# A transformer layer with product-key experts: the selection of two token blocks placed beside the start of the dense expert stage

## The chip, the cores and the metric

The kernel runs on one core of a Trainium2 chip. The metric is the device time of one execution in microseconds (us). The profile is that of one execution; its times count from the start of its span. The engines are TensorE (PE; its weight loads PEld), VectorE (DVE), ScalarE (ACT), GpSimd (POOL) and SyncE (SP), which here only issues DMA transfers.

## The reference

One layer over 1024 tokens of width 1024: two attentions (differential and chunked) whose gated outputs are merged and added to `x`, giving `h`; then a retrieval of experts; then a final norm.

```python
h = h + merged @ w_out
# peer(), on rmsnorm(h), for each token and each of 8 heads
s1, s2 = q[:, :, 0] . keys[:, 0], q[:, :, 1] . keys[:, 1]     # 128 keys each
v1, i1 = top_k(s1, 16);  v2, i2 = top_k(s2, 16)
sc, ci = top_k(v1[..., :, None] + v2[..., None, :], 16)
e = i1[ci // 16] * 128 + i2[ci % 16]                           # one of 16384 experts
g = softmax(sc)
a = gelu(u[e] . xb) * g
out = rmsnorm(h + sum(a * v[e]))
```

So every token uses 8 x 16 of 16384 experts, each a row of `u` and a row of `v`.

## The kernel before, in words

The 1024 tokens are eight blocks of 128. The front (projections, attentions, merge, queries) ends in `merge`, which leaves for each block the 16 best keys of either half (`vv`, `iu`), and in `choose` (called through `sel`), the *selection*: it adds the values to candidates (`cand`), takes the best 16 with `top16` (L558, on VectorE), and looks up the indices with one-hot products (`ohib`: a ScalarE cast at L611, VectorE at L612 to L619). Its exponential (L623) and small casts (`pf` at L587, `pos` at L602) run on ScalarE. For the blocks of `SBLK` it ends in `ei` (L639), the list of expert numbers.

The experts are done in two ways. For blocks 2 to 5 (`DBLK`) `dense_experts` computes all experts. The 16384 experts are 128 chunks of 128. It first transposes the normed tokens `xd` (L697, into the PSUM tile `trd`) and splits them into a high and a low part `x2h`, `x2l` (helper `split`, L126 on ScalarE and L127 on VectorE). For each chunk it loads a tile of `u` (`wr` in `wtile`) and one of `v` (`vr`), splits both (`wh`, `wl`, `vh`, `vl`), forms `ph` with 24 matmuls (`mm3`, L134), applies Gelu (L756), multiplies by the gate (`gj`, L757), splits the product (`ah`, `al`) and adds 24 more matmuls to the sums (`second` L710, `fourth` L717). `ph` has one buffer, `wh` and `wl` have two each. The gates have been written to DRAM tile by tile (`gst` to `gdr`, L673) by `gates`, and come back as `gj`, 16 transfers for four chunks. The end adds the sums to `h` (`hx`, L778) and applies the final norm (`final`, with the weights `wfd`).

For blocks 0, 1, 6 and 7 (`SBLK`) `experts` gathers 128 rows of `u` and 128 of `v` for each block by indirect DMA on GpSimd (L804), with one VectorE instruction for each (L810, L816). The dense stage and the gathers stand beside each other.

A scheduler puts the instructions of each engine into one fixed order, by the order in which the program states them and by when their inputs and their memory are free in its model of time. Engines wait for each other through semaphores. Memory comes from pools: a tile of a pool that is opened later can use the room of closed pools only when the last user of the tiles there is done. The pools `yza` and `tkp` (tiles of the selection), `fc`, `sm` and `psp` are in `fstack`; the end of the program reads:

```python
        with pool("gk") as gk:
            weave(mop(2, mp, yzb), 26, (gates(gk, d1), 32 * len(d1)))
            weave(mop(3, mp, yza), 26, (chain(sel([4, 5], yzb), gates(gk, d2)), 18 + 32 * len(d2)))
    run(sel([6, 7], yza))
    fstack.close()
    dense_experts()
    for b in SBLK:
        experts(b)
```

Of the kernel before, what the change touches and what calls it, by code (L numbers as in the profile page):

```python
# [7 lines left out]
F32 = mybir.dt.float32  # L8
# [7 lines left out]
P = 128  # L16
D = 1024
S = 1024
NB = S // P
KC = D // P  # L20
# [5 lines left out]
NCH = 128  # L26
# [6 lines left out]
DBLK = [2, 3, 4, 5]  # L33
# [33 lines left out]
def chain(*gens):  # L67
    for g in gens:
        yield from g
# [3 lines left out]
def layer_kernel(ctx, tc, x, w1, w_in, b_gate, lq1, lk1, lq2, lk2, subln, rel,  # L73
                 w_bd, w_bc, w_out, w2, wq, keyst, u, v, ut, wf, identd, dmd, iotad, out):
    nc = tc.nc
# [2 lines left out]
    gp = ctx.enter_context(tc.tile_pool(name="gath", bufs=GBUFS))  # L78
    sms = ctx.enter_context(tc.tile_pool(name="sms", bufs=2))
    wp = ctx.enter_context(tc.tile_pool(name="wp", bufs=2))  # L80
    drp = ctx.enter_context(tc.tile_pool(name="dr", bufs=1, space=bass.MemoryType.DRAM))

    def load(pool, shape, src, name):
# [53 lines left out]
    dsel = {}  # L137

    fstack = ExitStack()
    yza = fstack.enter_context(tc.tile_pool(name="yza", bufs=1))  # L140
    tkp = fstack.enter_context(tc.tile_pool(name="tkp", bufs=1))
    fc = fstack.enter_context(tc.tile_pool(name="fcon", bufs=1))
    sm = fstack.enter_context(tc.tile_pool(name="sm", bufs=4))
    psp = fstack.enter_context(tc.tile_pool(name="ps", bufs=2, space=PSUM))
# [536 lines left out]
    def dense_experts():  # L681
# [3 lines left out]
        with ExitStack() as st:  # L685
# [41 lines left out]
                    fourth(1, chunks)  # L727
                    chunks.clear()

            wfb = dk.tile([P, D], F32, name="wfd", bufs=1)  # L730
            nc.sync.dma_start(wfb, wf.to_broadcast([P, D]))
            hxs = []
            chunks = []
            new = None
            for j in range(NCH):
                if j == NCH - 2:
                    for b in DBLK[:2]:
                        hx = dk.tile([P, D], F32, name="hx", tag="hx", bufs=2)
                        nc.sync.dma_start(hx, hd[b])
                        hxs.append(hx)  # L740
                uw = wtile(ut[j])
                vr = dk.tile([P, D], F32, name="vr", tag="vr", bufs=RBUFS)
                nc.sync.dma_start(vr, v[j * P:(j + 1) * P, :])
                vh = dk.tile([P, D], F32R, name="vh", tag="vh", bufs=VBUFS)
                vl = dk.tile([P, D], F32R, name="vl", tag="vl", bufs=VBUFS)
                for hf in range(2):
                    cs = slice(hf * 512, hf * 512 + 512)
                    split(vr[:, cs], vh[:, cs], vl[:, cs])
                if j % JG == 0:
                    gj = dk.tile([P, T // TB, JG, TB], F32, name="gj", tag="gj")  # L750
                    for i in range(T // TB):
                        nc.sync.dma_start(gj[:, i], gdr[i][:, j:j + JG, :])
                ph = pd.tile([P, 512], F32, name="ph", tag="ph")
                mm3(ph, uw, (xh, xl), KC)
                ge = dk.tile([P, T], F32, name="ge", tag="ge")
                nc.scalar.activation(ge, ph, AF.Gelu)  # L756
                nc.vector.tensor_mul(ge.rearrange("p (n t) -> p n t", t=TB), ge.rearrange("p (n t) -> p n t", t=TB),  # L757
                                     gj[:, :, j % JG, :])
                ah = dk.tile([P, T], F32R, name="ah", tag="ah", bufs=ABUFS)
                al = dk.tile([P, T], F32R, name="al", tag="al", bufs=ABUFS)  # L760
                split(ge, ah, al)
                if new:
                    chunks.append(new)
                    sums(chunks)
                new = (j, (ah, al), (vh, vl))
            chunks.append(new)
            sums(chunks)
            for i, b in enumerate(DBLK):
# [120 lines left out]
    with pool("yzb") as yzb, pool("mp") as mp:  # L889
# [4 lines left out]
        with pool("gk") as gk:  # L894
            weave(mop(2, mp, yzb), 26, (gates(gk, d1), 32 * len(d1)))
            weave(mop(3, mp, yza), 26, (chain(sel([4, 5], yzb), gates(gk, d2)), 18 + 32 * len(d2)))
    run(sel([6, 7], yza))
    fstack.close()
    dense_experts()
    for b in SBLK:  # L900
        experts(b)
# [51 lines left out]
```

## Time and profile before

| | |
|---|---|
| median of three runs | 3437.65 us (3435.08 to 3438.16) |
| profiled execution | 3433.26 us, span 3431.5 us |
| mean granted TensorE clock in it | 0.944 |
| TensorE busy | 3085.0 us (90%) |
| VectorE busy | 2700.0 us (79%) |
| ScalarE busy | 1446.3 us (42%) |
| GpSimd busy | 1249.1 us (36%) |
| DMA, mean over the span | 288 GB/s |

The busy times are sums over the whole span, and stages with different limits are mixed in them, so the stretches of time are looked at one by one. A row of a timeline gives the start, the duration, the engine, the line, the tiles written and read, the shapes and, in brackets, how long the engine was idle before and what released it. Consecutive instructions overlap by a little, so the distance between two starts can be shorter than a duration. On SP's queue the duration is that of a row of issues, not of the transfers.

### The profile page before, as it was taken

To read this page: it belongs to the slowest core of one execution; us is meant where nothing else is said; L and a number is where in the kernel's file an instruction comes from. 1 tells how busy PE (TensorE), PEld (TensorE's weight loads), DVE (VectorE), ACT (ScalarE), POOL (GpSimd) and SP (SyncE) were. 2 spreads that over 40 slices of the span, in tenths; PEclk is the share of its full clock that TensorE was granted. 3 is DMA by queue.
4 is the path that set the end of the run, shared out by engine and by line. 5 is a ranking of instruction groups with operands and counts; after the bars stand their busy time and mean duration, and the time that the engine had idled before them with its cause. 6 is when DMAs were issued, how large, how long until landed. Compare 5 with 4: busy or idle time off the path is not lost.

```text
span 3431.5 us, 48288 instructions
## 1 busy us (share of the span) xinstructions
PE 3085.0 (90%) x16032; PEld 2551.8 (74%) x16032; DVE 2700.0 (79%) x5848; ACT 1446.3 (42%) x3029; POOL 1249.1 (36%) x1028
## 2 busy tenths in 40 slices
PE   7987699999979886987798359999999999999998
PEld 7986578888857654676677348888888888888886
DVE  4436897777779899987976978889998888999543
ACT  5634433434423544567669523333233333333332
POOL 0000455555544522344000144555555555555000
PEclk9999899999989987998898669999999999999999
DMA  7675999999999975898544499999999999999531
GB/s 240 219 244 189 374 333 348 333 352 334 326 340 351 324 236 186 281 360 331 203 162 157 145 343 319 346 350 339 347 345 345 346 342 344 346 340 349 166 123 49
DMA packets 406122, 987.13 MB, mean 288 GB/s; under 512 B 43184, under 2 KB 188400, under 8 KB 403696
## 3 DMA queue, kind: packets, MB, share of 16 engines
q0 software_dynamic: 147456, 536.94, 44.1%
q1 hardware_dynamic: 258416, 447.11, 37.4%
q8 instruction: 126, 2.06, 0.2%
q14 instruction: 124, 1.02, 0.1%
HBM read 905.72 MB, written 78.15 MB: 287 GB/s over the span
## 4 chain that ended last, share of the span: by engine, by line
PE 71%; issue 12%; DVE 7%; DMA 7%; ACT 2%; POOL 1%; SPq 0%; DVEq 0%; POOLq 0%; ACTq 0%
PE ph L134 20%; PE mm L134 16%; PE acc L710 15%; PE acc L717 5%; PE mm L490 5%; PE sc L347 3%; PE pv L372 3%; PE tr L203 2%; DMA ge<-in_u_dram,ei 2%; DVE junk L810 1%; DVE p L353 1%; POOL ge L804 1%; DMA rb<-rst 1%; DMA ge<-in_v_dram,ei 1%; DVE acc L816 1%
## 5 line engine op out<-in xcount | busy, mean ns | idle before, releaser
L804 POOL DMA_INDIRECT ge<-in_u_dram,ei x512 | 619.1, 1209 | 1249.0 <-DVE junk L810 396.4
L804 POOL DMA_INDIRECT ge<-in_v_dram,ei x512 | 629.8, 1230 | 683.2 <-DVE acc L816 462.0
L816 DVE SCALAR_TENSOR_TENSOR acc<-ge,a,acc 128x1024 f32<-128x1024 f32 x512 | 655.1, 1280 | 26.2 <-DMA ge<-in_v_dram,ei 20.1
L810 DVE SCALAR_TENSOR_TENSOR junk<-ge,xs 128x1024 bf16<-128x1024 f32 x512 | 624.7, 1220 | 53.7 <-DMA ge<-in_u_dram,ei 45.7
L127 DVE TENSOR_TENSOR wl<-wr,wh 128x1024 fp32r<-128x1024 f32 x232 | 283.6, 1223 | 233.1 <-ACT wh L126 107.5
L126 ACT CAST wh<-wr 128x1024 fp32r<-128x1024 f32 x232 | 243.7, 1051 | 406.5 <-PE ph L134 267.1
L134 PE MATMUL ph<-x2h,wh 128*128 128x512 f32 x1024 | 400.3, 391 | 11.8 <-ACT wh L126 10.4
L134 PE MATMUL ph<-x2l,wh 128*128 128x512 f32 x1024 | 399.9, 390 | 0.0
L134 PE MATMUL mm<-xh,wh 128*128 128x256 f32 (+1 forms) x1248 | 372.0, 325 | 0.7 <-ACT st L286 0.5
L134 PE MATMUL mm<-xl,wh 128*128 128x256 f32 (+1 forms) x1248 | 366.8, 321 | 1.4 <-DVE xl L232 1.3
L134 PEld LDWEIGHTS mm<-xh,wh 128*128 128x128 f32 x1248 | 236.9, 190 | 24.8 <-ACT st L286 2.3
L134 PE MATMUL ph<-x2h,wl 128*128 128x512 f32 x1024 | 253.1, 389 | 0.0
L134 PEld LDWEIGHTS mm<-xl,wh 128*128 128x128 f32 x1248 | 236.4, 190 | 21.5 <-DVE xl L232 2.1
L126 ACT CAST vh<-vr 128x512 fp32r<-128x512 f32 x256 | 140.4, 619 | 264.8 <-PE acc L717 243.4
L134 PE MATMUL mm<-xh,wl 128*128 128x256 f32 (+1 forms) x1248 | 234.4, 323 | 0.0
L134 PEld LDWEIGHTS ph<-x2h,wh 128*128 128x128 f32 x1024 | 193.2, 189 | 52.9 <-ACT wh L126 10.8
L134 PEld LDWEIGHTS ph<-x2l,wh 128*128 128x128 f32 x1024 | 193.2, 189 | 40.2
L134 PEld LDWEIGHTS ph<-x2h,wl 128*128 128x128 f32 x1024 | 192.3, 188 | 40.0
L347 PE MATMUL sc<-kt,qt 64*128 64x256 f32 (+3 forms) x608 | 202.1, 533 | 17.8 <-DVE mn L353 10.2
L710 PE MATMUL acc<-vh,ah 128*128 128x512 f32 x768 | 198.3, 389 | 0.0
L126 ACT CAST ah<-ge 128x512 fp32r<-128x512 f32 x128 | 79.7, 622 | 281.4 <-DVE ge L757 266.3
L134 PEld LDWEIGHTS mm<-xh,wl 128*128 128x128 f32 x1248 | 184.7, 189 | 16.8
(199 smaller groups left out, 5741.6 us busy)
## 6 DMA issues: line engine op xcount, KB each, us to landing
vr<-in_v_dram SPq DMA_DIRECT2D x128, 512.0 KB
wr<-in_ut_dram SPq DMA_DIRECT2D x128, 512.0 KB
wr<-in_w_in_dram SPq DMA_DIRECT2D x104, 512.0 KB
gdr<-gst SPq DMA_DIRECT2D x16, 2048.0 KB
gj<-gdr SPq DMA_DIRECT2D x512, 64.0 KB
wr<-in_w_bd_dram SPq DMA_DIRECT2D x40, 512.0 KB
wr<-in_w_out_dram SPq DMA_DIRECT2D x40, 512.0 KB
wr<-in_wq_dram SPq DMA_DIRECT2D x40, 512.0 KB
```

The lines of the kernel that those rows point to most:

```text
L126: nc.scalar.copy(hi, raw)
L127: nc.vector.tensor_sub(lo, raw, hi.bitcast(F32))
L134: nc.tensor.matmul(o, w[a][:, k, :], xx[b][:, k, :], start=(i == 0), stop=(i == last))
L203: nc.tensor.transpose(o[:, i * P:(i + 1) * P], s, ident)
L347: nc.tensor.matmul(o[:, :k1 - k0], q, k[:, k0:k1], start=True, stop=True)
L372: nc.tensor.matmul(o[:, :P], aT[:, j - c, :], vt[:, v0 + j, :], start=(j == 0), stop=(j == n - 1))
L490: nc.tensor.matmul(o, w[:, k, :], xx[:, k, :], start=(k == 0), stop=(k == K - 1))
L710: nc.tensor.matmul(acc[i][hf], a[x][:, i * P:(i + 1) * P], b[y][:, hf * 512:hf * 512 + 512], **kw)
L717: nc.tensor.matmul(o, aa[:, 3 * P:4 * P], bb[:, cs], start=(n == 0), stop=(n == len(todo) - 1))
L804: nc.gpsimd.indirect_dma_start(out=t, out_offset=None, in_=src, in_offset=bass.IndirectOffsetOnAxis(ap=ei[:, k:k + 1], axis=0))
L810: nc.vector.scalar_tensor_tensor(junk, t, 1.0, xs, op0=OP.mult, op1=OP.mult, accum_out=hid[:, k:k + 1])
L816: nc.vector.scalar_tensor_tensor(acc, t, a[:, k:k + 1], acc, op0=OP.mult, op1=OP.add)
```

## The change

The pools `yza` and `tkp` are opened at the start, outside `fstack`, and stay open to the end. `fstack` is closed before the selection of blocks 6 and 7 instead of behind it, so the room of that selection's tiles is never given to the dense stage. The dense stage no longer has tiles of its own for `wfd` and for the first two `hx`: they are loaded behind the loop over the chunks, into the weight buffers `wh` and `wl`, under the name `last`.

```diff
@@ -78,6 +78,8 @@
     gp = ctx.enter_context(tc.tile_pool(name="gath", bufs=GBUFS))
     sms = ctx.enter_context(tc.tile_pool(name="sms", bufs=2))
     wp = ctx.enter_context(tc.tile_pool(name="wp", bufs=2))
+    yza = ctx.enter_context(tc.tile_pool(name="yza", bufs=1))
+    tkp = ctx.enter_context(tc.tile_pool(name="tkp", bufs=1))
     drp = ctx.enter_context(tc.tile_pool(name="dr", bufs=1, space=bass.MemoryType.DRAM))
 
     def load(pool, shape, src, name):
@@ -137,8 +139,6 @@
     dsel = {}
 
     fstack = ExitStack()
-    yza = fstack.enter_context(tc.tile_pool(name="yza", bufs=1))
-    tkp = fstack.enter_context(tc.tile_pool(name="tkp", bufs=1))
     fc = fstack.enter_context(tc.tile_pool(name="fcon", bufs=1))
     sm = fstack.enter_context(tc.tile_pool(name="sm", bufs=4))
     psp = fstack.enter_context(tc.tile_pool(name="ps", bufs=2, space=PSUM))
@@ -727,17 +727,9 @@
                     fourth(1, chunks)
                     chunks.clear()
 
-            wfb = dk.tile([P, D], F32, name="wfd", bufs=1)
-            nc.sync.dma_start(wfb, wf.to_broadcast([P, D]))
-            hxs = []
             chunks = []
             new = None
             for j in range(NCH):
-                if j == NCH - 2:
-                    for b in DBLK[:2]:
-                        hx = dk.tile([P, D], F32, name="hx", tag="hx", bufs=2)
-                        nc.sync.dma_start(hx, hd[b])
-                        hxs.append(hx)
                 uw = wtile(ut[j])
                 vr = dk.tile([P, D], F32, name="vr", tag="vr", bufs=RBUFS)
                 nc.sync.dma_start(vr, v[j * P:(j + 1) * P, :])
@@ -763,6 +755,13 @@
                     chunks.append(new)
                     sums(chunks)
                 new = (j, (ah, al), (vh, vl))
+            def last(tag, src):
+                t = wp.tile([P, KC, P], F32, name="last", tag=tag).rearrange("p a b -> p (a b)")
+                nc.sync.dma_start(t, src)
+                return t
+
+            hxs = [last("wh", hd[b]) for b in DBLK[:2]]
+            wfb = last("wl", wf.to_broadcast([P, D]))
             chunks.append(new)
             sums(chunks)
             for i, b in enumerate(DBLK):
@@ -894,8 +893,8 @@
         with pool("gk") as gk:
             weave(mop(2, mp, yzb), 26, (gates(gk, d1), 32 * len(d1)))
             weave(mop(3, mp, yza), 26, (chain(sel([4, 5], yzb), gates(gk, d2)), 18 + 32 * len(d2)))
+    fstack.close()
     run(sel([6, 7], yza))
-    fstack.close()
     dense_experts()
     for b in SBLK:
         experts(b)
```

The scheduler's order moves with it. All that stands ahead of the places below is in the same order in both kernels. The lines of the helpers are two further down in the changed kernel: `split` is L128 and L129 there, `mm3` L136, and the Gelu L748.

VectorE, the end of the selection of block 7 (L637, L639) and the first `x2l`, before (`junk` at L810 is a gathered row):

```order
L810 SCALAR_TENSOR_TENSOR junk,hid<-ge,xs_28936 128x1024
L637 SCALAR_TENSOR_TENSOR row<-sel 128x128
L810 SCALAR_TENSOR_TENSOR junk,hid<-ge,xs_28936 128x1024
L639 CAST ei<-row 128x128
L810 SCALAR_TENSOR_TENSOR junk,hid<-ge,xs_28936 128x1024
L127 TENSOR_TENSOR x2l<-trd,x2h 128x4x128 x2
L810 SCALAR_TENSOR_TENSOR junk,hid<-ge,xs_28936 128x1024 x2
L127 TENSOR_TENSOR x2l<-trd,x2h 128x4x128 x2
L810 SCALAR_TENSOR_TENSOR junk,hid<-ge,xs_28936 128x1024
L127 TENSOR_TENSOR x2l<-trd,x2h 128x4x128 x2
L810 SCALAR_TENSOR_TENSOR junk,hid<-ge,xs_28936 128x1024
L127 TENSOR_TENSOR x2l<-trd,x2h 128x4x128
```

All `x2l` stand behind `ei` here.

VectorE, the first `x2l` in the changed kernel; `sv` and `ci` belong to the selection of block 6:

```order
L562 MAX sv<-cand 128x8
L129 TENSOR_TENSOR x2l<-trd,x2h 128x4x128
L562 MAX sv<-cand 128x8
L563 MAX_INDEX ci<-sv,cand 128x8 x2
L129 TENSOR_TENSOR x2l<-trd,x2h 128x4x128
L563 MAX_INDEX ci<-sv,cand 128x8 x5
L622 TENSOR_TENSOR g<-sv 128x128
L129 TENSOR_TENSOR x2l<-trd,x2h 128x4x128
L590 TENSOR_SCALAR s4u<-ci 128x128
L591 TENSOR_SCALAR s2u<-ci 128x128
L573 TENSOR_TENSOR cand<-vv 128x8x64
L576 TENSOR_TENSOR cand<-vv 128x8x48
```

The eight `x2l`, which stood behind all of the selection, now stand from the top 16 of block 6 on.

ScalarE, the same place, before:

```order
L602 CAST pos<-row 128x128
L611 CAST ohib<-iu 128x1024 x3
L126 CAST x2h<-trd 128x4x128 x7
L126 CAST vh<-vr 128x512 x2
L126 CAST x2h<-trd 128x4x128
L126 CAST wh<-wr 128x1024 x2
L126 CAST vh<-vr 128x512 x2
L756 ACT_TABLE_LOAD
L756 ACTIVATE ge<-ph 128x512
```

All `x2h` stand behind the selection. In the changed kernel:

```order
L128 CAST x2h<-trd 128x4x128 x3
L128 CAST vh<-vr 128x512 x2
L587 CAST pf<-ci 128x128
L128 CAST x2h<-trd 128x4x128
L623 ACT_TABLE_LOAD
L623 ACTIVATE g<-g 128x128
L594 CAST s_17269<-s4u 128x128
L595 CAST s_17270<-s2u 128x128
L128 CAST x2h<-trd 128x4x128
L128 CAST wh<-wr 128x1024
L602 CAST pos<-row 128x128
```

The casts into `x2h` were behind the last `ohib` cast of block 7 and are now ahead of, and between, the small casts of block 6.

VectorE a little later in the changed kernel, around the second `wl` (the cast and `wl` of chunk 1):

```order
L614 TENSOR_TENSOR ohib<-ohib 128x1024
L561 MATCH_REPLACE cand<-sv,cand 128x112 x5
L129 TENSOR_TENSOR x2l<-trd,x2h 128x4x128
L561 MATCH_REPLACE cand<-sv,cand 128x112
L129 TENSOR_TENSOR wl<-wr,wh 128x1024
L129 TENSOR_TENSOR vl<-vr,vh 128x512
L562 MAX sv<-cand 128x8
L603 TENSOR_TENSOR pos<-pf,s_17269 128x128
L129 TENSOR_TENSOR x2l<-trd,x2h 128x4x128
L562 MAX sv<-cand 128x8
```

The eighth `x2l` stands behind the second `wl`; before, it stood ahead of the first.

On SP's queue `rest`, `wfd`, `vr` and five `gj` stood ahead of the first `wr` of the stage; now it is `rest`, `vr` and nine `gj`, and seven `gj` and two `vr` stand between the first `wr` and the second. The order on GpSimd is the same; `ei` of block 6 stands on VectorE behind the fourth `wl`, that of block 7 behind the ninth, and the last gathered row behind the 116th `wl`, which was the 110th.

## Rows read from the trace of the kernel before

**Rows 1.** Busy time by stretch of time: the end of the front, the dense stage.

```profile
core 0: us, PE busy (x) PEld busy (x) DVE busy (x) ACT busy (x) POOL busy (x), PEclk, DMA share, GB/s
1900.00:1950.00 50.00, 18.64 (x106) 15.72 (x104) 49.37 (x276) 26.59 (x58) 0.00 (x0) 0.66 0.28 106
1950.00:2000.00 50.00, 0.00 (x0) 0.00 (x0) 42.56 (x93) 7.54 (x9) 30.39 (x25) 0.50 0.74 251
2029.00:2060.00 31.00, 31.00 (x137) 25.67 (x138) 24.04 (x37) 12.38 (x19) 8.56 (x8) 1.00 1.00 373
2800.00:3200.00 400.00, 400.00 (x1767) 331.20 (x1765) 359.59 (x428) 126.98 (x193) 207.94 (x162) 1.00 0.95 340
3200.00:3300.00 100.00, 100.00 (x443) 82.81 (x442) 41.87 (x59) 31.95 (x48) 0.00 (x0) 1.00 0.42 129
```

**Rows 2.** Timeline of TensorE; columns: start us, us, engine line op, tiles, shapes, idle before.

```profile
1922.91 1.10 PE L697 MATMUL trd<-ident,xd 128*128 128x128 f32 x8 [1.11 <-ACT gst L671]
2000.44 1.97 PE L697 MATMUL trd<-ident,xd 128*128 128x128 f32 x8 [76.43 <-DVE x2l L127]
...
2019.02 0.79 PE L134 MATMUL ph<-x2h,wh 128*128 128x512 f32 x1 [10.35 <-ACT wh L126]
...
2025.48 2.00 PE L134 MATMUL ph<-x2h,wl 128*128 128x512 f32 x8
...
2028.91 0.50 PE L134 MATMUL ph<-x2h,wh 128*128 128x512 f32 x1 [1.44 <-ACT ge L756]
...
2034.48 0.84 PE L710 MATMUL acc<-vh,ah 128*128 128x512 f32 x3
```

**Rows 3.** Timeline of ScalarE around the start of the dense stage.

```profile
1947.00 0.30 ACT L587 CAST pf<-ci 128x128 f32<-128x128 uint32 x1 [10.99 <-DVE ci L563]
...
1998.79 1.07 ACT L126 CAST x2h<-trd 128x512 fp32r<-128x512 f32 x2 [13.53 <-DVE ei L639]
...
2017.92 1.04 ACT L126 CAST wh<-wr 128x1024 fp32r<-128x1024 f32 x1 [6.10 <-DMA wr<-in_ut_dram]
...
2024.03 1.04 ACT L126 CAST wh<-wr 128x1024 fp32r<-128x1024 f32 x1 [5.07 <-DMA wr<-in_ut_dram]
```

**Rows 4.** Busy time by stretch: after the last gate tile is written out.

```profile
1931.00:1932.00 1.00, 0.00 (x0) 0.00 (x0) 1.00 (x10) 0.00 (x0) 0.00 (x0) 0.50 0.04 16
```

**Rows 5.** Timeline of VectorE: the selection of blocks 6 and 7, first dense chunk.

```profile
1930.85 0.45 DVE L562 MAX8 sv<-cand 128x8 f32<-128x112 f32 x2
...
1942.67 0.27 DVE L562 MAX8 sv<-cand 128x8 f32<-128x112 f32 x1
...
1950.91 0.69 DVE L612 TENSOR_TENSOR ohib<-pos,iotaj 128x1024 bf16<-128x1024 bf16 x1
...
1954.07 0.69 DVE L612 TENSOR_TENSOR ohib<-pos,iotaj 128x1024 bf16<-128x1024 bf16 x1
...
1962.30 1.22 DVE L810 SCALAR_TENSOR_TENSOR junk<-ge,xs 128x1024 bf16<-128x1024 f32 x1 [1.36 <-DMA ge<-in_u_dram,ei]
...
2010.94 1.28 DVE L127 TENSOR_TENSOR vl<-vr,vh 128x512 fp32r<-128x512 f32 x2
...
2019.00 1.23 DVE L127 TENSOR_TENSOR wl<-wr,wh 128x1024 fp32r<-128x1024 f32 x1 [5.03 <-ACT wh L126]
```

**Rows 6.** Timeline of the queue of SP: issues of loads of the dense stage.

```profile
2004.95 0.33 SPq L194 DMA_DIRECT2D wr<-in_ut_dram  x1
2007.36 12.53 SPq L752 DMA_DIRECT2D gj<-gdr  x11
2019.98 0.38 SPq L194 DMA_DIRECT2D wr<-in_ut_dram  x1
...
2021.84 0.90 SPq L752 DMA_DIRECT2D gj<-gdr  x2
```

**Rows 7.** Timelines of TensorE and VectorE at the end of the kernel.

```profile
3403.55 1.98 PE L134 MATMUL ph<-x2h,wl 128*128 128x512 f32 x8
...
3413.95 3.67 DVE L778 TENSOR_TENSOR hx<-hx,acc 128x512 f32<-128x512 f32 x6 [0.22 <-PE acc L710]
```

## The prediction

> **What bounds the kernel now.** I read the busy time by stretch first [rows 1]. From 2029 us TensorE is busy without a gap, 31.00 of 31 us to 2060 and 400.00 of 400 between 2800 and 3200, at full granted clock: the dense stage is bound by TensorE, and its end moves one for one with its start unless something starves it. VectorE is nearly as full there (359.59 of 400), because it also works off the gathered experts; after 3200 GpSimd does nothing more and VectorE is 42% busy, so the gathered half ends well over 100 us before the dense half.
>
> The hole lies just ahead of that stage: 18.64 us of TensorE work between 1900 and 1950, none between 1950 and 2000 [rows 1]. TensorE's timeline names it [rows 2]: the first transposes of the dense stage run at 1922.91, the next ones wait 76.43 us, and the first `ph` matmul starts at 2019.02. ScalarE's timeline says what ends the wait: the first cast into `x2h` waits for `ei` on VectorE [rows 3], the last instruction of the selection of block 7. The data for the cast had been there since 1924; it waited for the memory that the selection's pools gave back. So 76 us of TensorE time are lost to an allocation, and the VectorE work in that hole could stand beside TensorE work.
>
> **The change, part by part.** In the new order the casts into `x2h` stand on ScalarE ahead of the selection's first `pf` cast, and the `x2l` differences sit between the selection's instructions on VectorE. What now sets the start of TensorE is a race of three chains.
>
> *Release of memory.* The dense tiles now take the room of pools that close earlier, the gate tiles `gst` among them, and these must first have been written out. Transfers fall to 16 GB/s in the stretch from 1931 to 1932 [rows 4], so I let the first `x2h` cast start at 1931.2 instead of 1998.79 [rows 3]. Not before 1924 in any case (the transposes).
>
> *VectorE.* The first matmul of chunk 0 reads all of `x2h` and `x2l`, so it waits for the eighth `x2l`, which stands behind the second `wl`. The selection's instructions that stand ahead of it ran in the kernel before from the end of the row at 1930.85 to the row at 1942.67, 11.4 us [rows 5]. Between them there are now eight `x2l`, five `vl` and two `wl`: thirteen at 0.64 (1.28 for two) and two at 1.23 [rows 5], 10.8 us. 1931.2 + 22.2 gives 1953.4, about 1953.5.
>
> *Loads.* The second `wl` needs the second weight tile. On SP's queue the first stands behind `rest`, `vr` and nine `gj`, the second behind seven more `gj` and two `vr`. A `gj` issue took between 0.45 (two in 0.90) and 1.14 us (eleven in 12.53), a weight load 4.05 us from its issue at 2019.98 to its cast at 2024.03, and 12.97 from 2004.95 to 2017.92 [rows 3, 6]. Low: 16 x 0.45 + six others at 0.4 + 4.05 = 13.7, so 1945. High: 16 x 1.14 + 2.4 + 12.97 = 33.6, so 1965. The high values come from a time at which the gathers of block 6 used the same DMA engines; now no gather runs until the selection of block 6 is done, so I take a value near the low end, 1949, the rest for transfers that wait on each other. Cast, `wl`, a `vl` and small instructions follow, 4.5 us: the eighth `x2l` at 1953.5, level with the VectorE chain. The Trainium skill, *DMA: Bandwidth & Descriptors*, section "Queues, rings and completion order", says that a DMA engine takes packets in turn from every queue with work, which is a reason for the quick landing here; by that page alone I would take 1945 and a gain of 64 us at the second `ph`, by the row at the same place of the stage 1965 and 48 (both worked out below); the trace shows both prices, not the turns.
>
> With some waiting between the three chains I put the first `ph` at 1955. Its 24 matmuls took 8.4 us after the pause (16 in 6.46 us, eight in 2.00) [rows 2], hence 1963.4. The second `ph` needs the Gelu of the first, since there is one `ph` buffer. It came 1.4 us later before [rows 2]; now block 7's `pf`, three small instructions, a 1.04 us `ohib` cast and the third `wh` cast stand ahead of the Gelu on ScalarE. `pf` is not late: the selection between the first `L562` row of the block and `pf` took 4.3 us [rows 3, 5], three `vl` more make 6.2, so 1961. The third `wh`, though, waits until the first `ph` has left its buffer free: 1.04, and the 1.4 us of table load and Gelu that lay there before, with the hand-overs some 3 us. Second `ph` at 1966.5, where it was 2028.91 [rows 2]: **62.4 us earlier**.
>
> *The next chunks.* The rest of block 7 (four `ohib` rounds) spreads over some six chunks. A round took at most 3.16 us from one `L612` to the next [rows 5], 12.6 in all, 2.1 per chunk. VectorE carries 90% of a chunk of 10.9 us (48 matmuls; 1767 in 400 us) [rows 1], 9.8 us; the sum of 11.9 is 1.0 us over what TensorE needs. Six chunks: 6 us at most, less what the double buffers have in hand. I charge 4 us (between 0 and 10).
>
> *End of the gathers.* `ei` of block 6 is written some 20 to 25 us later, but the same VectorE work is done until the end. The last gathered sum stands six dense chunks later in VectorE's order, 116 instead of 110 of 128. That leaves 12 chunks, some 130 us. Nothing.
>
> *The tail.* `wfd` and the two `hx` loads leave the start of the stage, 1.5 MB less among the loads there (`wfd` stood ahead of `vr`; the two `hx` came later). They return as `last` into the weight buffers: two can start when chunk 126's `ph` has read its weights, the third when chunk 127's has, at 3405.5 in the old time [rows 7]. With the 4.05 us of a load it is there at 3409.6, and the first addition that needs one runs at 3413.95 [rows 7]. With the 12.97 us of the slow row it would be 4.5 us late; DMA is nearly idle there, so nothing.
>
> *Sum.* 62.4 less 4 gives 58.4 us. The profiled execution took 3433.26 us (span 3431.5), so 3374.9; the median of the three runs lies 4.4 us above that execution, and I forecast for the median: 3437.65 - 58.4, **3379 us**. Bounds of the terms: with the weight tile at 1945 VectorE's chain alone holds, `ph` 1953.5 and no stall later, 64 us, and hardly more if `x2h` needs not wait for the gate transfer, since the first `x2l` stands behind the selection's row at 1930.85; with 1965 the first `ph` is at 1969.5, the second at 1981, 48 us, and with 10 us of stalls 38. So 3374 to 3400 from these alone.
>
> **The rivals.**
> *Queues lock into each other.* ScalarE and VectorE work in order, and each `ohib` round crosses between them behind casts that wait for TensorE or for a load. If every one of the ten first chunks loses 4 us in this way, the gain is 62.4 - 40, 22 us: 3415. For it: eight of these crossings stand among the first chunks' casts, and VectorE has only 1.1 us a chunk free. Against: the `wh` and `wl` of the next chunk have a buffer of their own, and TensorE had no idle time at all between 2029 and 2060 [rows 1], with gathers between the casts that VectorE has to wait for at times (1.36 us at 1962.30) [rows 5].
>
> *The change costs time.* The same stalls, but long enough that TensorE's clock falls between the bursts. The mean granted clock was 0.66 in the stretch with 37% of TensorE work and 1.00 in the full ones [rows 1]; a matmul at the start of the first chunk took 0.40 us (1.2 GHz, the last few already faster), one of the second chunk 0.232 (2.4 GHz, 24 in 5.57) [rows 2]. A chunk of 48 matmuls would then take 8.1 us more. Eight chunks in that state lose 65 us, the whole gain; ten lose 81, and the time is 3437.65 - 62.4 + 81, 3456. It decides from a loss of about 6 us a chunk. Against it: the one gap that the trace has inside the dense stage's start, 1.44 us, left the clock where it was [rows 2]. The Trainium skill, *TensorE: Matmul & The Clock Gate*, section "HAM oscillation — how this bites in real kernels", describes this pattern, bursts of matmuls divided by waits that each start at half rate again; here it would give 3456, and the trace agrees only in that the first burst after the hole is slow.
>
> *The change doesn't do it.* If `x2h` still had to wait for the selection through some other tile, the time would stay at 3438. Against: the casts stand on ScalarE ahead of `pf` of block 6, so they cannot wait for anything behind it.
>
> **How the numbers follow.** Forecast (38 to 66 us gained) 0.81; queues that lock (10 to 38 us) 0.11; no effect 0.02; slower through stalls and clock 0.04; gained more than 66 us, through something that I don't see, 0.02. The range of 8 in 10 is the forecast with its bounds, opened by a little on both sides since the loads are the least known: 3366 to 3404. A measurement of this kernel tells about 0.2%, 6.9 us, from no change. Faster 0.94, same 0.02, slower 0.04.
>
> **What would show it.** In the profile after: the first `x2h` cast near 1931 and released by a transfer (the release chain right) or at 1924 (wrong, by 7 us at the start, though VectorE's chain then holds); the first `ph` between 1953 and 1970, waiting for `x2l`; a pause of about 3 us ahead of the second `ph`; few and short TensorE pauses in the next ten chunks, with full clock; the first gather at 1975 to 1990; `ei` of block 7 around the ninth chunk; the last gathered sum some 130 us ahead of the end; no pause for `last` ahead of the final additions. The prediction is wrong if TensorE shows pauses of several us in each of the first ten chunks, if the clock falls there, or if pauses appear later in the stage, where VectorE has 10% to spare.

## The result and the profile after

| | before | after |
|---|---|---|
| median | 3437.9 us (four runs, 3435.08 to 3441.82) | 3394.09 us (four runs, 3385.27 to 3403.12) |
| ratio of after to before | | 0.9868, 95% interval 0.9844 to 0.9891 |
| profiled execution, span | 3433.26, 3431.5 us | 3385.27, 3383.5 us |
| TensorE busy | 3085.0 us (90%) | 3101.4 us (92%) |
| mean granted clock | 0.944 | 0.955 |

The change gained 43.8 us; 58.4 were forecast. The predicted 3379 us is 15 us too low; the result lies within the range of 3366 to 3404. Two numbers in the table don't fit together: TensorE does the same matmuls at a higher mean clock, and yet is busy for 16 us more.

The busy time by stretch shows that the hole is gone, and where the rest went. These are the rows that answer to [rows 1], with the first stretch that is free of waits, 1989 to 2060:

```profile
core 0: us, PE busy (x) PEld busy (x) DVE busy (x) ACT busy (x) POOL busy (x), PEclk, DMA share, GB/s
1900.00:1950.00 50.00, 21.99 (x105) 16.93 (x105) 49.96 (x241) 29.94 (x61) 0.00 (x0) 0.66 0.69 243
1950.00:2000.00 50.00, 47.79 (x195) 38.38 (x194) 44.08 (x105) 21.82 (x32) 15.41 (x14) 0.93 0.66 228
1989.00:2060.00 71.00, 71.00 (x311) 57.92 (x310) 67.24 (x115) 22.40 (x33) 37.36 (x30) 1.00 0.94 334
2800.00:3200.00 400.00, 400.00 (x1740) 326.31 (x1739) 356.13 (x427) 120.55 (x182) 209.53 (x166) 1.00 0.96 339
3200.00:3300.00 100.00, 100.00 (x436) 81.49 (x435) 44.11 (x59) 36.08 (x57) 0.00 (x0) 1.00 0.43 133
```

Between 1950 and 2000 TensorE works for 47.79 us, where it did nothing. But between 2800 and 3200 it is full, at full granted clock, and does 1740 matmuls instead of 1767; between 3200 and 3300, with GpSimd idle and less than half of the DMA load, 436 instead of 443. Something makes a matmul slower, and neither clock, wait nor gathers is it.

The start itself came about as forecast. TensorE's timeline, to set beside [rows 2]:

```profile
1917.88 1.10 PE L697 MATMUL trd<-ident,xd 128*128 128x128 f32 x8 [1.12 <-ACT gst L671]
1927.13 1.11 PE L697 MATMUL trd<-ident,xd 128*128 128x128 f32 x4 [8.15 <-DVE x2l L129]
...
1948.07 0.80 PE L136 MATMUL ph<-x2h,wh 128*128 128x512 f32 x1 [6.60 <-DVE x2l L129]
...
1954.17 2.02 PE L136 MATMUL ph<-x2h,wl 128*128 128x512 f32 x8
1958.41 0.50 PE L136 MATMUL ph<-x2h,wh 128*128 128x512 f32 x1 [2.21 <-ACT ge L748]
...
1959.91 0.59 PE L136 MATMUL ph<-x2h,wh 128*128 128x512 f32 x1
1960.30 0.63 PE L136 MATMUL ph<-x2l,wh 128*128 128x512 f32 x1
1960.73 0.63 PE L136 MATMUL ph<-x2h,wh 128*128 128x512 f32 x1
...
1963.29 0.43 PE L136 MATMUL ph<-x2h,wh 128*128 128x512 f32 x1
...
3368.02 0.39 PE L717 MATMUL acc<-vh,al 128*128 128x512 f32 x1
```

The second `ph` starts at 1958.41 instead of 2028.91 [rows 2], 70.5 us earlier. 5.0 of these are not the change's: the front, whose order is the same, ended earlier in this execution (first transposes at 1917.88, before at 1922.91). From the transposes to the second `ph` it is 40.5 us where it was 106.0, so 65.5 us come from the change. From the second `ph` to the last matmul, though, it is 3368.02 - 1958.41 = 1409.6 us where it was 3416.01 - 2028.91 = 1387.1. These 22.5 us are the part of the gain that is missing: 5.0 + 65.5 - 22.5 = 48.0, the difference of the two spans.

What is slower is seen in TensorE's groups by tiles between 2800 and 3200 (in each row: count, busy us, mean ns of one). Before:

```profile
L134 PE MATMUL ph<-x2h,wh 128*128 128x512 f32 x296 | 115.1, 389 | 0.0
L134 PE MATMUL ph<-x2l,wh 128*128 128x512 f32 x296 | 115.1, 389 | 0.0
L134 PE MATMUL ph<-x2h,wl 128*128 128x512 f32 x296 | 73.1, 389 | 0.0
L710 PE MATMUL acc<-vh,ah 128*128 128x512 f32 x222 | 57.8, 389 | 0.0
...
L717 PE MATMUL acc<-vh,al 128*128 128x512 f32 x74 | 28.8, 389 | 0.0
```

After:

```profile
L136 PE MATMUL ph<-x2l,wh 128*128 128x512 f32 x291 | 115.3, 396 | 0.0
L136 PE MATMUL ph<-x2h,wh 128*128 128x512 f32 x291 | 114.6, 394 | 0.0
L136 PE MATMUL ph<-x2h,wl 128*128 128x512 f32 x288 | 72.8, 394 | 0.0
...
L710 PE MATMUL acc<-vh,ah 128*128 128x512 f32 x216 | 56.3, 389 | 0.0
...
L717 PE MATMUL acc<-vh,al 128*128 128x512 f32 x74 | 29.1, 393 | 0.0
```

Every group of matmuls into `ph` is slower (389 to about 395 ns); those into `acc` are not, but for `acc<-vh,al` of L717 (393), many of which are the last before a row of matmuls into `ph`; the last section comes back to them. Since these durations overlap, the time from start to start is worked out from the counts: 400 / 1767 = 0.2264 us before, 400 / 1740 = 0.2299 on average now. Half of a chunk's 48 matmuls go into `ph`; if these alone are slower, one takes 2 x 0.2299 - 0.2264 = 0.2334 us. 24 x 128 of them by 0.0070 make 21.5 us, nearly all of the 22.5. Same instruction, same shape, same clock: what differs is where `x2h` and `x2l` lie. As `yza` and `tkp` stay open below it, the dense pool begins 21,024 bytes higher in each partition, `x2h` at byte 110,720 instead of 89,696. The weight tiles stay where they were (`wh` at 81,504, `wl` at 73,312, and 4096 further the second of each).

### The profile page after: what moved, and what is told of

Its sections match the earlier page's. It is cut to its first block, busy times and chain, and to the rows that moved or that the text cites. A ratio compares the mean times of both kernels' runs of the same rounds, so it can differ in the third digit from the quotient of the medians.

```text
span 3383.5 us, 48294 instructions
## 1 busy us (share of the span) xinstructions
PE 3101.4 (92%) x16032; PEld 2548.4 (75%) x16032; DVE 2696.5 (80%) x5848; ACT 1445.1 (43%) x3029; POOL 1249.5 (37%) x1028
## 4 chain that ended last, share of the span: by engine, by line
PE 75%; DVE 12%; DMA 5%; ACT 4%; issue 3%; POOL 1%; SPq 0%; DVEq 0%; POOLq 0%; ACTq 0%
PE ph L136 21%; PE mm L136 17%; PE acc L710 15%; PE mm L490 7%; PE acc L717 5%; PE sc L347 3%; PE pv L372 3%; PE tr L203 2%; DVE junk L809 1%; DMA ge<-in_u_dram,ei 1%; PE gg L669 1%; DVE acc L815 1%; DVE qs L561 1%; DVE iu L563 1%; DVE iu L560 1%
## 5 line engine op out<-in xcount | busy, mean ns | idle before, releaser
L129 DVE TENSOR_TENSOR wl<-wr,wh 128x1024 fp32r<-128x1024 f32 x232 | 283.4, 1222 | 215.8 <-ACT wh L128 110.7
L128 ACT CAST wh<-wr 128x1024 fp32r<-128x1024 f32 x232 | 243.4, 1049 | 404.8 <-PE ph L136 276.5
L136 PE MATMUL ph<-x2h,wh 128*128 128x512 f32 x1024 | 406.2, 397 | 8.8 <-DVE x2l L129 6.6
L136 PE MATMUL ph<-x2l,wh 128*128 128x512 f32 x1024 | 407.7, 398 | 0.0
L136 PE MATMUL mm<-xh,wh 128*128 128x256 f32 (+1 forms) x1248 | 372.1, 325 | 0.7 <-ACT st L286 0.6
L136 PE MATMUL mm<-xl,wh 128*128 128x256 f32 (+1 forms) x1248 | 367.0, 321 | 1.3 <-DVE xl L232 1.2
L136 PE MATMUL ph<-x2h,wl 128*128 128x512 f32 x1024 | 259.4, 395 | 0.0
L136 PEld LDWEIGHTS mm<-xh,wh 128*128 128x128 f32 x1248 | 237.0, 190 | 24.8 <-ACT st L286 3.1
L128 ACT CAST vh<-vr 128x512 fp32r<-128x512 f32 x256 | 140.0, 618 | 269.3 <-PE acc L717 244.5
L136 PEld LDWEIGHTS mm<-xl,wh 128*128 128x128 f32 x1248 | 236.6, 190 | 21.4 <-DVE xl L232 2.0
L136 PEld LDWEIGHTS ph<-x2h,wh 128*128 128x128 f32 x1024 | 193.4, 189 | 55.5 <-DVE x2l L129 7.0
L136 PE MATMUL mm<-xh,wl 128*128 128x256 f32 (+1 forms) x1248 | 234.5, 324 | 0.0
L136 PEld LDWEIGHTS ph<-x2l,wh 128*128 128x128 f32 x1024 | 193.6, 189 | 47.7
L136 PEld LDWEIGHTS ph<-x2h,wl 128*128 128x128 f32 x1024 | 192.0, 188 | 46.9
L128 ACT CAST ah<-ge 128x512 fp32r<-128x512 f32 x128 | 79.7, 622 | 294.9 <-DVE ge L749 294.9
L136 PEld LDWEIGHTS mm<-xh,wl 128*128 128x128 f32 x1248 | 184.8, 190 | 16.8
```

The lines of the kernel that those rows point to most:

```text
L128: nc.scalar.copy(hi, raw)
L129: nc.vector.tensor_sub(lo, raw, hi.bitcast(F32))
L136: nc.tensor.matmul(o, w[a][:, k, :], xx[b][:, k, :], start=(i == 0), stop=(i == last))
```

## The experiments

Three theories of the 21 us: **T1**, the distance between the moving operand (`x2h`, `x2l`) and the stationary one (`wh`, `wl`) counts, modulo some power of two; **T2**, the region of memory in which `x2h` lies counts, or **T4** its own place in a stretch of 2048 bytes; **T3**, the other engines' traffic in the new order. The tool is an unused tile in front of another one, set to zero once by GpSimd and read by nobody. No instruction of the dense stage changes. An address below is the start in a partition, as the program's allocation gives it; distances are counted from `wh` to `x2h` (those of the other pairs of `x2h`, `x2l`, `wh` and `wl` are the same modulo 2048). From one matmul of a chunk to the next `x2h` moves on by 2048 bytes and `wh` by 512, so only what is left of a distance modulo 512 is common to all of them. The ratio given with a run is to the kernel before, run beside it on the same chip (medians 3436.75 to 3442.21 us).

**The changed kernel with 32 bytes ahead of `x2h`** (with 1504, 96, 480 or 224 in the runs further down):

```diff
+            pad = dk.tile([P, 8], F32, name="pad", bufs=1)
+            nc.gpsimd.memset(pad, 0.0)
             xh = dk.tile([P, KC, T], F32R, name="x2h", bufs=1)
```

> The changed kernel with an unused tile of 32 bytes per partition ahead of x2h: x2h starts at 110752 instead of 110720, everything behind it in that pool 32 bytes higher, the weight tiles wh and wl stay at 81504 and 73312. In the changed kernel a ph matmul takes 0.2330 us from start to start (0.2265 in the kernel before), 48 of a chunk 11.03 us (10.87), 1740 in the 400 us from 2800 (1767). Theory T1, the alignment of x2h and x2l against the stationary tiles within 64 bytes sets the rate (before both were at 32 in 64, after 0 and 32): ph back to 0.2265, some 21 us faster than the changed kernel, about 3373 us. Rival T2, the region of the memory in which x2h lies: unchanged, 0.233 and 3394. Rival T3, the load of the other engines and transfers in the dense stage: unchanged.

Measured: 3383.82 us (ratio to the kernel before 0.9843, 0.9826 to 0.9859), 1756 matmuls between 2800 and 3200. None of the three expectations: moving the tile by 32 bytes gives back about half of the loss. That excludes T2 and T3 as they were put, and T1 with a modulus of 64.

**With 1504 bytes**, the distance of the kernel before, but 22 KB higher:

> The changed kernel with an unused tile of 1504 bytes per partition ahead of x2h: x2h at 112224, which stands in a stretch of 2048 bytes where it stood in the kernel before (1632), and as wh does. T1 with any modulus up to 2048: ph 0.2265, about 3373 us. T2 (region): the tile is still 22 KB higher than before, so unchanged, 0.233 and 3394. T3: unchanged.

Measured: 3375.95 us (0.9823, 0.9806 to 0.9839). The groups are those of the kernel before:

```profile
L136 PE MATMUL ph<-x2h,wh 128*128 128x512 f32 x296 | 115.1, 389 | 0.0
L136 PE MATMUL ph<-x2l,wh 128*128 128x512 f32 x296 | 115.1, 389 | 0.0
L136 PE MATMUL ph<-x2h,wl 128*128 128x512 f32 x296 | 73.1, 389 | 0.0
```

**The kernel before with 544 bytes**, the same diff with `[P, 136]`: old order of the work, new distance.

> The kernel before with an unused tile of 544 bytes per partition ahead of x2h: x2h at 90240, which is 128 in a stretch of 2048 bytes as in the changed kernel (before 1632). T1: ph from 0.2265 to 0.233, 128 chunks of 0.16 us more, about 21 us slower, 3459. T2: unchanged, 3438. T3: unchanged, 3438.

Measured: 3460.65 us, slower by a ratio of 1.0062 (1.0045 to 1.0079), and the rows of the changed kernel appear in the kernel before:

```profile
2800.00:3200.00 400.00, 400.00 (x1740) 325.92 (x1739) 356.38 (x434) 120.05 (x182) 210.67 (x168) 1.00 0.95 338
```

From the second `ph` to the last matmul it took 1411.1 us, against 1387.1 without the 544 bytes. So the loss needs neither the overlap nor the new order.

**The 1504 bytes behind `x2l`**, as a control:

```diff
             xl = dk.tile([P, KC, T], F32R, name="x2l", bufs=1)
+            pad = dk.tile([P, 376], F32, name="pad", bufs=1)
+            nc.gpsimd.memset(pad, 0.0)
```

> The changed kernel with an unused tile of 1504 bytes per partition behind x2l: x2h and x2l stay where the change put them, all tiles behind them move by 1504 bytes as in the run with that tile ahead. A control: T1, T2 and T3 all expect 0.233 and 3394; if it turns out faster, the place of x2h is not the cause but that of a tile behind it (rest, vr, vh, vl, gj, ge, ah, al).

Measured: 3400.1 us (0.9889, 0.9873 to 0.9906), 1732 matmuls. It stays slow, so moving the tiles behind `x2h` and `x2l` does not give the loss back. It adds a little: from the second `ph` to the last matmul it took 1415.8 us, against 1409.6 in the changed kernel, and here `ah` and `al` stand 32 bytes off a multiple of 256 from `x2h`. Why that costs 6 us is open.

**Which modulus, and whose place.** Two further distances, and a run that moves the weights too:

> The changed kernel with 96 unused bytes ahead of x2h: x2h at 110816, which is 640 bytes past a multiple of 2048 counted from wh (change 544, with 32 bytes 576, before and with 1504 bytes 0). 0 gave 0.2265 us from ph to ph (1767 and 1766 matmuls in 2800 to 3200), 576 about 0.229 (1756), 544 about 0.233 (1740). T1a, the distance counts modulo 128 (544 is 32, 576 is 64, 640 is 0): 0.2265, 1766 matmuls, some 3376 us. T1b, the distance counts modulo 512 or more: not full speed, 1756 or fewer, 3384 or more.

> The changed kernel with 480 unused bytes ahead of x2h: x2h 1024 bytes past a multiple of 2048 counted from wh, 0 modulo 128, 512 and 1024. T1a (modulo 128): full speed, 1766 matmuls, some 3376 us. T1c, modulo 512 or 1024: the same. T1d, modulo 2048 only: slower, 1756 or fewer, 3384 or more. Where the run with 96 bytes is slow and this one fast, the modulus is 256 to 1024.

```diff
     wp = ctx.enter_context(tc.tile_pool(name="wp", bufs=2))
+    wpad = wp.tile([P, 136], F32, name="wpad", bufs=1)
+    nc.gpsimd.memset(wpad, 0.0)
...
+            pad = dk.tile([P, 376], F32, name="pad", bufs=1)
+            nc.gpsimd.memset(pad, 0.0)
             xh = dk.tile([P, KC, T], F32R, name="x2h", bufs=1)
```

> The changed kernel with 544 unused bytes at the start of the pool of the weight tiles and 1504 ahead of x2h: wh and wl are moved to 128 in a stretch of 2048 bytes, x2h to 128 too, the place at which the changed kernel and the kernel before with 544 bytes were slow. T1, the place of x2h against the weight tile counts: full speed, 1766 matmuls, some 3376 us. Rival T4, the place of x2h itself counts, wherever the weights lie: 0.233, 1740 matmuls, 3394 to 3400 us.

Measured: 96 bytes 3394.82 us (0.9871, 0.9855 to 0.9888), 1737 matmuls; 480 bytes 3375.09 (0.9805, 0.9789 to 0.9822), 1766; weights moved as well 3375.73 (0.9814, 0.9797 to 0.983), 1767. The last one settles T4: `x2h` lies at the place in 2048 bytes at which two kernels were slow, and runs at full speed because the weights lie there too.

> The changed kernel with 224 unused bytes ahead of x2h: x2h 768 bytes past a multiple of 2048 counted from wh, 256 past one of 512. So far distances of 0 and 1024 gave full speed (0.2265 us, 1766 matmuls in 2800 to 3200), 544, 576 and 640 did not (1740, 1756, 1737). Modulus 256: full speed, 1766 matmuls, some 3376 us. Modulus 512: slower, 1756 or fewer, 3384 to 3395 us.

Measured: 3372.32 us (0.9796, 0.9781 to 0.9812), and

```profile
2800.00:3200.00 400.00, 400.00 (x1767) 331.20 (x1766) 363.47 (x434) 124.22 (x188) 210.05 (x165) 1.00 0.96 342
```

A distance of 256 is as good as 0, and one of 640, 128 modulo 256, was slow: the modulus is 256. The runs so far together, from their traces ("start" is from the first transposes to the second `ph`, "stage" from there to the last matmul):

| kernel | distance mod 256 | matmuls, 2800 to 3200 | start us | stage us | median us |
|---|---|---|---|---|---|
| before | 0 | 1767 | 106.0 | 1387.1 | 3437.9 |
| before, 544 bytes | 32 | 1740 | 106.9 | 1411.1 | 3460.65 |
| after | 32 | 1740 | 40.5 | 1409.6 | 3394.09 |
| after, 1504 behind `x2l` | 32 | 1732 | 41.5 | 1415.8 | 3400.1 |
| after, 32 bytes | 64 | 1756 | 40.6 | 1397.2 | 3383.82 |
| after, 96 bytes | 128 | 1737 | 40.8 | 1411.3 | 3394.82 |
| after, 224 bytes | 0 | 1767 | 41.1 | 1388.7 | 3372.32 |
| after, 480 bytes | 0 | 1766 | 42.1 | 1389.7 | 3375.09 |
| after, 1504 bytes | 0 | 1766 | 41.2 | 1388.8 | 3375.95 |
| after, weights moved too | 0 | 1767 | 41.1 | 1388.7 | 3375.73 |

The two columns "start" and "stage" separate cleanly: the order of the work sets the one, the distance the other.

**Is it a matter of `x2h` alone?** 544 bytes ahead of `ah`, the stationary operand of `acc`, in the kernel with 480 bytes:

```diff
+                if j == 0:
+                    apad = dk.tile([P, 136], F32, name="apad", bufs=1)
+                    nc.gpsimd.memset(apad, 0.0)
                 ah = dk.tile([P, T], F32R, name="ah", tag="ah", bufs=ABUFS)
```

> The changed kernel with x2h where it is fast (480 unused bytes ahead of it: 3375 us, 1766 matmuls in 2800 to 3200) and 544 unused bytes ahead of ah and al, the stationary tiles of the acc matmuls: these stood a multiple of 256 bytes from vh and vl, now 32 bytes past one. If the distance counts for every pair of a moving and a stationary tile: acc from 0.2265 to some 0.233 us, 24 a chunk over 128 chunks by 0.0065, 20 us slower, 3395 us, some 1740 matmuls, with ph unchanged. Rival, it is something about x2h and the weight tiles alone (their 2 KB steps from one matmul to the next): unchanged, 3375 us, 1766.

Measured: 3401.95 us (0.9893, 0.9877 to 0.991), 1737 matmuls, and now it is the matmuls into `acc` that are slow:

```profile
L136 PE MATMUL ph<-x2l,wh 128*128 128x512 f32 x293 | 114.4, 390 | 0.0
L136 PE MATMUL ph<-x2h,wh 128*128 128x512 f32 x292 | 114.1, 391 | 0.0
...
L712 PE MATMUL acc<-vh,ah 128*128 128x512 f32 x216 | 57.6, 395 | 0.0
L712 PE MATMUL acc<-vh,al 128*128 128x512 f32 x216 | 56.3, 396 | 0.0
```

So the distance counts for both pairs of the stage. The loss of 27 us in the medians is 7 more than expected, but from the second `ph` to the last matmul it took 1411.4 us against 1389.7, 21.7 more, close to the 20 expected. 390 and 391 ns show that `ph` lost a little too, and why is open.

**Only the loads.** The kernel before with `wfd` and the first two `hx` moved to the end as `last`, and nothing else:

```diff
-            wfb = dk.tile([P, D], F32, name="wfd", bufs=1)
-            nc.sync.dma_start(wfb, wf.to_broadcast([P, D]))
...
+            hxs = [last("wh", hd[b]) for b in DBLK[:2]]
+            wfb = last("wl", wf.to_broadcast([P, D]))
```

> One part of the change alone, on the kernel before: wfd and the two hx loads leave the start of the dense stage and come at its end as last, the pools are closed in the old order, x2h stays where it was. By the prediction's terms (start nothing while the selection holds it, tail nothing): 3437, within 3 us of the kernel before. Rival, the late loads hold the final additions: up to 4.5 us slower, 3441. If it were 10 us faster or more, part of what the change gave would be the loads' and not the overlap's.

Measured: 3435.1 us, ratio 0.998 (0.997 to 0.999), 4.7 us faster where 3 at most were expected. A small gain, and not nothing: the start is 103.0 us instead of 106.0, likely because `wfd` is no longer loaded beside the first `vr` and `wr`; that is argued from the order of the loads, not shown by itself. The tail is the same, 15.5 us from the start of the last matmul to the end of the span in both.

**Both ends.** The projections at the start of the program read `xh`, `xl` against the same weight tiles. Beside the kernel with 480 bytes, run once more:

```diff
+        xpad = xp.tile([P, 16 if gi else 48], F32, name="xpad", tag="xpad")
+        nc.gpsimd.memset(xpad, 0.0)
         xh = xp.tile([P, KC, T], F32R, name="xh", tag="xh")
```

> The changed kernel with 480 unused bytes ahead of x2h once more, beside the next kernel on the same chip: 3375 us as before, between 3370 and 3380.

> The changed kernel with 480 unused bytes ahead of x2h and, in the projections at the start of the program, with 64 and 192 unused bytes ahead of the two xh tiles, so that these too stand a multiple of 512 from the weight tiles (now 448 and 256 modulo 512). There an mm matmul of 512 columns takes 0.240 us from start to start (0.2265 for a ph), one of 256 columns 0.123 (0.113 for half of it). Theory T1 for these matmuls too: 1248 of 512 columns by 0.013 and 2496 of 256 columns by up to 0.0094, 16 to 40 us less TensorE work, of which what TensorE bounds arrives at the end: 3340 to 3365 us, and about 0.227 a matmul of 512 columns. Rival: these matmuls are slow for another reason (the clock, which was 0.95 there, and other matmuls between them): unchanged, 3375 us and 0.240.

Measured: 3375.35 us for the 480 bytes (0.9806, 0.9792 to 0.9819), 3374.9 us with both (0.9808, 0.9795 to 0.9821): no gain. The groups before 1400 us, first with 480 bytes alone:

```profile
L136 PE MATMUL mm<-xh,wh 128*128 128x256 f32 x832 | 204.0, 285 | 0.5 <-ACT st L286 0.5
...
L136 PE MATMUL mm<-xl,wh 128*128 128x512 f32 x416 | 165.5, 398 | 0.0
```

and with both:

```profile
L136 PE MATMUL mm<-xh,wh 128*128 128x256 f32 x832 | 207.1, 287 | 0.5 <-ACT st L288 0.5
...
L136 PE MATMUL mm<-xl,wh 128*128 128x512 f32 x416 | 163.7, 393 | 0.0
```

The sums cancel, and the means hide two opposite effects. With a modulus of 256 only one of the two `xh` had been off, by 192: that of blocks 2 to 7, whose projections have matmuls of 512 and of 256 columns. The other, at 0 modulo 256 in both kernels, is read by matmuls of 256 columns alone. Rows of the timeline of the first, with 480 bytes alone:

```profile
501.04 1.07 PE L136 MATMUL mm<-xh,wl 128*128 128x256 f32 x8
...
505.68 2.03 PE L136 MATMUL mm<-xh,wl 128*128 128x512 f32 x8
```

and with both:

```profile
500.93 1.12 PE L136 MATMUL mm<-xh,wl 128*128 128x256 f32 x8
...
505.54 1.98 PE L136 MATMUL mm<-xh,wl 128*128 128x512 f32 x8
```

From start to start, as a median of the traces between 400 and 1000 us, a matmul of 512 columns went from 233 to 227 ns, the 0.227 that T1 expected. One of 256 columns went from 114 to 120, the time that those of the other `xh` take before 300 us in both kernels. So at a distance of 0 these matmuls of 512 columns are faster and those of 256 slower; why the short ones are is open. The expected 16 to 40 us were wrong in the price of a matmul of 512 columns (0.013 us a matmul expected, 0.006 by the medians) and in the sign for the short ones.

## Why the prediction was right, and where it was wrong

**The cause of the hole, right.** Memory, not data, held the first cast. With the pools kept open it ran 7.5 us after the transposes and not behind the selection, at the same time as `rest` on SP's queue. ScalarE, to compare with [rows 3], and SP's queue, with [rows 6]:

```profile
1925.34 1.07 ACT L128 CAST x2h<-trd 128x512 fp32r<-128x512 f32 x2 [7.51 <-DVE cand L561]
...
1941.23 1.04 ACT L128 CAST wh<-wr 128x1024 fp32r<-128x1024 f32 x1
```

```profile
1925.22 0.32 SPq L703 DMA_DIRECT2D rest<-hd  x1
1925.59 0.42 SPq L735 DMA_DIRECT2D vr<-in_v_dram  x1
1926.06 4.79 SPq L744 DMA_DIRECT2D gj<-gdr  x9
1930.95 0.38 SPq L194 DMA_DIRECT2D wr<-in_ut_dram  x1
1931.37 3.28 SPq L744 DMA_DIRECT2D gj<-gdr  x7
1934.69 0.91 SPq L735 DMA_DIRECT2D vr<-in_v_dram  x2
1935.70 0.38 SPq L194 DMA_DIRECT2D wr<-in_ut_dram  x1
```

From the transposes to the cast: 8.3 us forecast, 7.5 measured. The bracket names VectorE, which had an instruction end there by chance; the `rest` issue 0.1 us earlier waited for the same memory, and that it is the write of the last gate tile is inferred from the order, not shown by itself.

**VectorE's chain, right.** 22.2 us from the cast to the end of the eighth `x2l` were forecast, and it is 22.7 (1925.34 to 1948.01), behind the second `wl` as the order said:

```profile
1944.38 0.68 DVE L129 TENSOR_TENSOR x2l<-trd,x2h 128x512 fp32r<-128x512 f32 x1
...
1945.22 1.21 DVE L129 TENSOR_TENSOR wl<-wr,wh 128x1024 fp32r<-128x1024 f32 x1
...
1947.33 0.68 DVE L129 TENSOR_TENSOR x2l<-trd,x2h 128x512 fp32r<-128x512 f32 x1
```

**The loads, right and a little better.** A `gj` issue took 0.53 us (nine in 4.79) and 0.47 (seven in 3.28), the low end. The second weight tile was there by 1941.23, 23.4 us after the transposes, where 26.1 were forecast; its cast follows the one before it without a wait. The Trainium skill, *DMA: Bandwidth & Descriptors*, section "Queues, rings and completion order", which let engines take packets in turn from every queue, was the ground for 64 us at the second `ph`; 65.5 lies nearer to it than to the 62.4 of the text, but the loads did not set the start here, and no run shows engines taking turns.

**Burst and pause.** The first burst ran 8.1 us (8.4 forecast), the pause was 2.21 (3). In sum the second `ph` came 40.5 us after the transposes instead of 43.6: the shift was 65.5, not 62.4. By the run with the loads alone, 3 of the 106.0 us of the kernel before were owed to the loads that moved; whether the changed kernel would lose as much with them in the old place is not shown.

**Stalls in the next chunks: 4 forecast, none seen.** From the second `ph` to the end TensorE waited once, for that Gelu:

```profile
PE ph L136 <- ACT ge L748: 2.2, 1, 2.2
```

With the right distance the stage takes 1388.7 us in two kernels of the table, 1.6 more than before. After the pause the clock fell for eight matmuls, from 1959.91 to 1963.29 (granted clock 0.58 between 1960 and 1964), which took some 0.42 us from start to start as at 1.2 GHz: eight by 0.2 is 1.6. The kernel with 224 bytes does the same behind its pause of 2.78 us. The prediction had a pause of 3 us and put nothing for the clock, since 1.44 us had left it where it was. The rival of queues that lock falls, and so does the one that is slower through stalls and clock: the granted clock is 1.00 from 1989 to 3360. What the Trainium skill, *TensorE: Matmul & The Clock Gate*, section "HAM oscillation — how this bites in real kernels", describes shows once and only in part: the burst behind the pause began at full rate, fell to half for eight matmuls, and no second one did so.

**Gathers and tail, right.** The first gather starts at 1971.59, which is 1976.6 counted from the transposes of the execution before (forecast 1975 to 1990), and GpSimd has ended by 3200. The last gathered sum starts at 3206, 177 us ahead of the end, where some 130 were forecast. The three `last` loads don't hold the end:

```profile
3343.96 0.33 SPq L760 DMA_DIRECT2D last<-hd  x1
3345.82 0.33 SPq L760 DMA_DIRECT2D last<-in_wf_dram  x1
3355.69 0.32 SPq L760 DMA_DIRECT2D last<-hd  x1
```

```profile
3365.95 2.48 DVE L777 TENSOR_TENSOR last<-last,acc 128x512 f32<-128x512 f32 x4 [0.22 <-PE acc L710]
```

The additions wait 0.22 us for TensorE, as in [rows 7].

**The step that failed** is the one in the first paragraph that had no number: "its end moves one for one with its start unless something starves it". Nothing starved TensorE, and still the stage became 22.5 us longer. 1.6 of these are the clock behind the pause, the other 20.9 come from the distance: the change moved `x2h` and `x2l` by a number of bytes that is no multiple of 256, and a matmul into `ph` took 0.233 us instead of 0.226. The diff shows that the pool begins somewhere else; the prediction put a tile's address at nothing, without a reason. Put right, the sum reads 65.5 - 1.6 = 63.9 for the order of the work, less 20.9 (1409.6 - 1388.7) for the address: 43.0 in the profiled executions, 43.8 in the medians. The kernels with the right distance have the first term alone: in the medians they are 61 to 70 us faster than the kernel before beside them. That the range held is luck: it is owed to its upper half, which was left open for slow loads and stalls that did not come, and a loss that the prediction did not know of fell into it.

The version that beats both kernels is the changed one with 224 or 480 unused bytes ahead of `x2h`: 3372 to 3375 us, some 20 us faster than the change as it was made. The two cannot be told apart, their medians lie within each other's spread.

## What to carry to other kernels

A change of pools also moves tiles. When TensorE is full at full clock and does fewer matmuls in a fixed stretch than before, compare the mean duration of the same group of matmuls in both kernels, and then the distance of its two operands in memory. Here an unused tile of 224, 480 or 1504 bytes, by which moving and stationary operand start a multiple of 256 bytes apart, was worth a third as much as the whole overlap. That is for matmuls of 512 columns; for those of 256 columns in the projections the same step was a loss, so try it and measure.

## What the runs showed of the hardware that was not expected

Here the time of a matmul of 512 columns from start to start depends on the distance between its moving and its stationary operand in a partition, modulo 256 bytes: 0.226 us at 0, about 0.229 at 64 (2 x 400 / 1756 - 0.2264), about 0.233 to 0.234 at 32 and 128 (1740 and 1737 matmuls in 400 us). The weight loads themselves read the same in the traces, 188 ns on average at any distance. The Trainium skill, *TensorE: Matmul & The Clock Gate*, section "Step-by-step: what each phase is for", says that loading the next weights takes no read bandwidth from the running matmul, since each has a read port of its own. Here the same two streams cost each other about 3% at some distances and nothing at others; the measurement decides. That the two reads meet in the same part of the memory is a likely reason, but it is argued only: no run shows which of them waits, and in this stage other distances than 0, 32, 64 and 128 were not tried. In the projections a matmul of 512 columns took 233 ns at 192 and 227 at 0, one of 256 columns 114 and 120.

Which weights count, those of the matmul itself or those of the next, is seen where matmuls into `acc` and into `ph` meet. In the changed kernel the load for the next matmul starts 2 to 4 ns behind the start of the running one (rows around 3001 us). The last matmul into `acc` before one into `ph` took 0.235 us to the next start there, while all others in its row took 0.226 to 0.227 (means, 2300 to 3250 us): its own operands, `vh` and `al`, stand right, and `wh`, loaded meanwhile, does not stand right to `vh`. With the tile behind `x2l`, where it does, it took 0.227 to 0.229. So there the distance to the *next* matmul's weights counts. With `ah` moved the same matmul took 0.232 to 0.236 although `wh` stands right to `vh`, and the first matmuls behind a slow row were slow too in some runs, so this is not the whole rule.

The front, with its instructions in one order, ended anywhere between 1917.88 and 1931.85 us (first transposes) in the kernels that left it as it was. This is not much less than the effect of the distance; times of single executions are compared here from the transposes on for that reason.
